# Attention in three score visits a pair, with one value product a pair from packed turned weights, and small operations joined

## The chip, the cores and the metric

One core of a Trainium2 chip runs the whole kernel. The time is what one execution takes on the device, in microseconds (us); the numbers below are medians of several executions, and one more execution was taken with the hardware profiler on. The core's engines work side by side and meet at semaphores: TensorE (PE) multiplies matrices into PSUM, eight banks of 128 x 512 float32; VectorE (DVE) and ScalarE (ACT) read PSUM and do elementwise work; GpSimd (POOL) fills and makes masks; SyncE's queue (SP) issues the large loads. Each engine works through its instructions in order.

## The reference

Two decoder layers on 512 tokens of width 1024, in float32. Layer 0 has an attention mixer with 16 heads of 64, layer 1 a gated short convolution; each is followed by a gated MLP of width 2816 with a causal width-3 convolution. Only the attention is touched:

```python
proj = rms_norm(h, norm_g) @ w_in          # q, k, v of 16 heads and 8 forget logits
q_fox = rms_norm(q[:, :H_FOX], fox_q_g)    # likewise k_fox, q_sb, k_sb: per head
# heads 0-7, forgetting attention
logits = q @ k.T * dh ** -0.5 + cum_f[q] - cum_f[k]
o = softmax(where(key_pos <= q_pos, logits, -inf)) @ v
# heads 8-15, stick-breaking attention
z = q @ k.T * dh ** -0.5
log_one_minus = where(key_pos < q_pos, log_sigmoid(-z), 0)
later = reverse_cumsum(log_one_minus) - log_one_minus
o = where(key_pos < q_pos, exp(log_sigmoid(z) + later), 0) @ v
h = h + concat(o_fox, o_sb) @ w_out
```

A block of 128 queries needs only the keys up to its own end: 128, 256, 384 and 512 of them.

## The kernel before

**Number form.** Products need more than one pass of the 32-bit matmul format, so each operand is split into a high and a low part (tiles `*_hi`, `*_lo`): ACT copies to the high part, DVE subtracts it. `mm3` (L246) issues high x high, low x high, high x low; `load` (L210) does the same for weights when they arrive. A value product takes the weights of the softmax in two parts against a `v` tile that holds high and low side by side in 128 columns (L482).

**Pairs and visits.** Heads go in pairs `p` = 0..7 (0 to 3 forgetting, "fox"; 4 to 7 stick-breaking), the two heads on 64 partitions each. `logits(p, b)` (L597) is one visit: the scores of query block `b` for both heads, one PSUM bank each of the four with tag "b", then the softmax, or two sigmoids and a reverse product scan, into tiles `w`. With 64 rows a matmul uses half of the array, and the two heads' matmuls run side by side. The smallest width is 256 columns. `turn(p, b, ws)` (L645) transposes the weights on PE in a bank of tag "c" (two banks) and splits them into `pt` tiles, which hold 256 queries for each of 4 key blocks, with the part after the diagonal filled with zeros by GpSimd (L653). `weigh(p, half)` (L666) multiplies 256 queries with `v` into a bank of tag "a" (two banks) and adds the two column halves for each head into `o`.

**Fillers.** `queries_keys(p)` (L520) and `values(g)` (L482) are generators that project queries, keys and values of later pairs, into banks of tag "a". After its two sums, `queries_keys` has a chain: squares summed on PE (`sums`, L533), turned (`turned_sums`, L545), inverse root on DVE (`rsqrt`, L318), spread and turned again (`rows`, L571). `output(g, done)` (L692), also with tag "a", is half of the output projection; `output_begin` (L718) starts the last half in banks of tag "b".

**Order of the work.** The order is written out in Python: `fill(us)` (L192) adds to a quota and draws that much planned PE time from the fillers, `spend` (L179) moves a planned clock, and `after(us, fn)` (L184) issues a step when that clock has gone on so far. `SUMS, FLAT, ROWS` (L45) are the delays of the chain above, `FILL1, FILL2, BEFORE` (L47) the quotas around a visit. The main loop (L839) issues for each g the scores of block g, `FILL1`, the product of a half that was turned an iteration before, the turn of block g - 1, and `FILL2`. The compiler may still exchange instructions of one engine where their operands are ready at other times.

Of the kernel before, what the change touches and what calls it, by code (L numbers as in the profile page):

```python
# [25 lines left out]
P = 128  # L26
# [18 lines left out]
SUMS, FLAT, ROWS = 3.0, 1.5, 5.0  # L45
NSUMS, NROWS, LATE = 4.0, 3.0, 7.0
FILL1, FILL2, BEFORE = 1.0, 2.6, 2.0  # L47
# [3 lines left out]
def trunk(  # L51
# [24 lines left out]
    blank = tiny.tile([P, P], BF16, tag="blank", name="blank", bufs=1)  # L76
# [3 lines left out]
    xin_scope = ExitStack()  # L80
    xin = xin_scope.enter_context(tc.tile_pool(name="xin", bufs=1))
# [177 lines left out]
    class Norm:  # L259
# [25 lines left out]
        def scale(self, sums):  # L285
            v = tiny.tile([P, NB], F32, tag="nv", name=f"nv_{self.name}")
# [31 lines left out]
    def rsqrt(dst, v, n, name):  # L318

        def t(tag, dt=F32):  # L320
            return tiny.tile([P, n], dt, tag=f"{tag}{n}", name=f"{tag}_{name}")
# [49 lines left out]
    for g, ps_ in enumerate(((1, 2), (3, 4), (5, 6), (7,))):  # L371
# [110 lines left out]
    def values(g):  # L482
# [3 lines left out]
        for b in range(NB):  # L486
            acc = bank("a")
# [19 lines left out]
    rx2 = const.tile([P, NB], F32, tag="rx2", name="rx2")  # L507

    def square_norm():
        dve.tensor_tensor(rx2, norm.col, norm.col, op=ALU.mult)  # L510
        dve.tensor_scalar(rx2, rx2, 1.0 / HD, None, op0=ALU.mult)
# [8 lines left out]
    def queries_keys(p):  # L520
# [3 lines left out]
        v = tiny.tile([P, NB, 2, 2], F32, tag="qv", name=f"qv{p}")  # L524
        r = tiny.tile([P, NB, 2, 2], F32, tag="qr", name=f"qr{p}")
# [7 lines left out]
        def sums():  # L533
# [7 lines left out]
            flat = work.tile([P, 2 * P], F32, tag="flat", name=f"flat{p}", bufs=1)  # L541
# [3 lines left out]
        def turned_sums(t, flat):  # L545
            for i in range(2):
                pe.transpose(t[:, (2 + i) * P:(3 + i) * P], flat[:, i * P:(i + 1) * P], ident)
            spend(0.25)
            dve.tensor_tensor(
                v, t[:, 2 * P:4 * P].rearrange("p (i b c) -> p b i c", i=2, b=NB)[:, :, :, 0:2],  # L550
                rx2[:, :, None, None].to_broadcast([P, NB, 2, 2]), op=ALU.mult,
            )
            scales()

        def scales():
            vf, rf = (t.rearrange("p b i h -> p (b i h)") for t in (v, r))
            dve.tensor_scalar(vf, vf, EPS, None, op0=ALU.add)
            rsqrt(rf, vf, 16, f"qk{p}")
            rf = r.rearrange("p b i h -> p b (i h)")
            dve.tensor_tensor(rf, rf, norm.col[:, :, None].to_broadcast([P, NB, 4]), op=ALU.mult)  # L560
            if not fox:
                s = q_scale[p] = aw.tile([P, 2, NB, 2], F32, tag="qscale", name=f"qscale{p}", bufs=3)
                dve.tensor_copy(s[:, 0], r[:, :, 1, :])
                dve.tensor_scalar(s[:, 1], r[:, :, 1, :], -1.0, None, op0=ALU.mult)
            wides = {}
            for i in kept:
                wides[i] = work.tile([P, S], F32, tag="u0", name=f"qwide{p}{i}").rearrange("p (b h d) -> p b h d", b=NB, h=2)
                dve.tensor_copy(wides[i], r[:, :, i, :][:, :, :, None].to_broadcast([P, NB, 2, HD]))
# [12 lines left out]
        for i in range(2):  # L581
            acc = bank("a")
# [14 lines left out]
    def logits(p, b):  # L597
# [5 lines left out]
        n = (b + 1) * P  # L603
        wide = max(n, 256)
        tok = slice(b * P, n)
        ss = [bank("b") for _ in range(2)]
        for step, (ql, kl) in enumerate(((q_hi, k_hi), (q_hi, k_lo), (q_lo, k_hi))):
            for e in range(2):
                rows = slice(e * HD, (e + 1) * HD)
                pe.matmul(ss[e][:, 0:wide], ql[rows, tok], kl[rows, 0:wide], start=step == 0, stop=not fox and step == 2)  # L610
        if fox:
            for e in range(2):
                rows = slice(e * HD, (e + 1) * HD)
                pe.matmul(ss[e][:, 0:wide], dl[rows, p, tok], dr[rows, 0:wide], start=False, stop=False)
            for e in range(2):
                pe.matmul(ss[e][:, tok], ident16, mask, start=False, stop=True)
        spend((4 if fox else 3) * wide * 0.00044 + (0.12 if fox else 0))
        ws = []
        for e in range(2):
            s = ss[e]  # L620
            w = aw.tile([P, S], F32, tag="w", name=f"w{p}{b}{e}", bufs=WB)
            ws.append(w)
            if fox:
                top = tiny.tile([P, 1], F32, tag="top", name=f"top{p}{b}{e}")
                dve.reduce_max(top, s[:, 0:n], axis=AX.X, negate=True)
                total = tiny.tile([P, 1], F32, tag="total", name=f"total{p}{b}{e}")
                act.activation(w[:, 0:n], s[:, 0:n], AF.Exp, bias=top, accum_out=total)
                inv = tiny.tile([P, 1], F32, tag="inv", name=f"inv{p}{b}{e}")
                dve.reciprocal(inv, total)
                dve.tensor_scalar(w[:, 0:n], w[:, 0:n], inv, None, op0=ALU.mult)  # L630
            else:
                scale = q_scale[p]
                rest = aw.tile([P, S], F32, tag="rest", name=f"rest{p}{b}{e}")
                act.activation(rest[:, 0:n], s[:, 0:n], AF.Sigmoid, scale=scale[:, 1, b, e:e + 1])
                act.activation(w[:, 0:n - 1], s[:, 0:n - 1], AF.Sigmoid, scale=scale[:, 0, b, e:e + 1])

                pool.memset(w[:, n - 1:n], 0.0)
                back = rest[:, 1:n][:, ::-1]
                dve.tensor_tensor_scan(back, back, begin[:, S - n + 1:S][:, ::-1], 0.0, op0=ALU.mult, op1=ALU.max)  # L639
                dve.tensor_tensor(w[:, 0:n - 1], w[:, 0:n - 1], rest[:, 1:n], op=ALU.mult)  # L640
        return ws
# [3 lines left out]
    def turn(p, b, ws):  # L645

        half, n = b // 2, (b + 1) * P
        if b % 2 == 0:
            pts[p, half] = []
            for e in range(2):  # L650
                both = [aw.tile([P, NB, 256], F32R, tag=f"pt{i}", name=f"pt{p}{half}{e}{i}", bufs=PT) for i in range(2)]
                for t in both:
                    pool.memset(f32(t[:, 2 * half + 1, 0:P]), 0.0)  # L653
                pts[p, half].append(both)
        at_ = slice((b % 2) * P, (b % 2 + 1) * P)
        for e in range(2):
            t = bank("c")
            for k in range(b + 1):
                pe.transpose(t[:, k * P:(k + 1) * P], ws[e][:, k * P:(k + 1) * P], ident)  # L659
            src = t[:, 0:n].rearrange("p (k q) -> p k q", q=P)  # L660
            hi, lo = pts[p, half][e]
            act.activation(hi[:, 0:b + 1, at_], src, AF.Copy)
            dve.tensor_tensor(lo[:, 0:b + 1, at_], src, f32(hi[:, 0:b + 1, at_]), op=ALU.subtract)
        spend(0.22 * (b + 1))

    def weigh(p, half):  # L666
# [4 lines left out]
        acc = bank("a")  # L671
        to = slice(half * 256, (half + 1) * 256)
        last = 2 * half + 1
        for e in range(2):
            hi, lo = pts[p, half][e]
            for k in range(last + 1):
                w = v[:, k, 2 * (p % 2) + e].rearrange("p i d -> p (i d)")
                pe.matmul(acc[:, e * 256:(e + 1) * 256], w, hi[:, k, :], start=k == 0, stop=False)
                pe.matmul(acc[:, e * 256:(e + 1) * 256], w, lo[:, k, :], start=False, stop=k == last)
        spend(0.44 * (last + 1))  # L680
        if p == 4 and half == 0:
            o_tiles[1] = mixed(1)
        o_hi, o_lo = o_tiles[p // 4]
        total = work.tile([P, S], F32, tag="y", name=f"o{p}{half}")[:, 0:256]
        for e in range(2):
            own, other = (slice(i * HD, (i + 1) * HD) for i in (e, 1 - e))
            cols = slice(e * 256, (e + 1) * 256)
            act.activation(total[own, :], acc[other, cols], AF.Copy)
            dve.tensor_tensor(total[own, :], acc[own, cols], total[own, :], op=ALU.add)  # L689
        split(o_hi[:, p % 4, to], o_lo[:, p % 4, to], total)  # L690
# [120 lines left out]
    after(NORM0, lambda: (norm.scale(sums0), square_norm()))  # L811
# [6 lines left out]
    aw = attn.enter_context(tc.tile_pool(name="aw", bufs=2))  # L818

# [5 lines left out]
    dr = ap_.tile([P, S], F32R, tag="dr", name="dr")  # L825
# [6 lines left out]
    for g, ps_ in enumerate(((1, 2), (3, 4), (5, 6), (7,))):  # L832
# [3 lines left out]
    blocks = [(p, b) for p in range(8) for b in range(NB)]  # L836
    waiting = {}
    fill(PRE)
    for g in range(len(blocks) + 2):  # L839
        if g < len(blocks):  # L840
            waiting[g] = logits(*blocks[g])
            fill(FILL1)
        if g == len(blocks):
            fillers.append(output_begin())
            fill(BEFORE)
        if g >= 2 and blocks[g - 2][1] % 2:
            p, b = blocks[g - 2]
            weigh(p, b // 2)
            if (p, b) == (3, 3):
                fillers.append(output(0, residual))  # L850
        if 1 <= g <= len(blocks):
# [161 lines left out]
```

## Time and profile before

| | us |
|---|---|
| median of 3 runs | 1221.25 (1220.8 to 1221.3) |
| profiled execution, its own time | 1220.77 |
| its span, first to last instruction | 1219.0 |
| PE busy in the span | 1204.0 |
| DVE, ACT, POOL busy | 762.8, 503.4, 26.6 |
| attention stage, roughly | 35 to 285 us of the span |

In the profile's rows, a line such as L610 is a line of the kernel; PE stands for matmuls and PEld for their weight loads. The end of a matmul is modelled, so the time of one is best read from the start of one to the start of the next. Tiles stand by name without their buffer numbers: psa, psb and psc are PSUM banks of the tags "a", "b" and "c".

### The profile page before, as it was taken

Reading aid. Unit: us, or ns where it says so; the run is one execution under the profiler, and the core shown is the slowest. Engines: PE = TensorE matmul, PEld = TensorE weight load, DVE = VectorE, ACT = ScalarE, POOL = GpSimd, SP = SyncE. Lnnn points to the kernel's source line nnn. Section 1 sums busy time; section 2 is a strip of 40 time slices with the busy share of each in tenths; the row PEclk is TensorE's granted clock in tenths of the full one; section 3 lists DMA queues with packets and bytes.
Section 4 is the critical chain, followed back from the end, with each engine's and each line's share of the span. In section 5 each row is a group of like instructions: output and inputs, shape, how many; then the busy total and the mean of one; then the engine's idle time right before and its main releaser. Section 6 shows DMA issues by size and latency. Waiting matters only on the chain.

```text
span 1219.0 us, 15006 instructions
## 1 busy us (share of the span) xinstructions
PE 1204.0 (99%) x5841; PEld 973.4 (80%) x5841; DVE 762.8 (63%) x1250; ACT 503.4 (41%) x787; POOL 26.6 (2%) x139
## 2 busy tenths in 40 slices
PE   8999999999999999999999999999999999999998
PEld 7887877778888888888888888888888888888886
DVE  5887888887867777663333555465776767672222
ACT  6556576655544443432222222233434344442120
POOL 4000000000000000000000000000000000000000
PEclk9999999999999999999999999999999999999999
DMA  7312121213233333323333333323233332322330
GB/s 196 88 36 70 36 69 36 70 62 96 87 102 89 97 93 94 96 81 93 94 95 104 89 102 87 104 87 104 87 93 98 89 102 87 103 87 88 121 102 35
DMA packets 182696, 108.14 MB, mean 89 GB/s; under 512 B 4732, under 2 KB 175020, under 8 KB 182624
## 3 DMA queue, kind: packets, MB, share of 16 engines
q1 hardware_dynamic: 182080, 106.94, 29.7%
q8 instruction: 46, 0.75, 0.3%
q0 software_dynamic: 384, 0.17, 0.1%
q14 instruction: 26, 0.21, 0.1%
q10 hardware_dynamic: 160, 0.07, 0.0%
HBM read 105.06 MB, written 2.10 MB: 88 GB/s over the span
## 4 chain that ended last, share of the span: by engine, by line
PE 91%; DVE 6%; ACT 2%; issue 1%; DMA 0%; SPq 0%; DVEq 0%; POOL 0%; ACTq 0%
PE psa L248 13%; PE psa L250 12%; PE psa L249 12%; PE psb L248 12%; PE psb L250 12%; PE psb L249 12%; PE psa L503 2%; PE psa L504 2%; PE psa L505 2%; PE psb L504 2%; PE psb L503 2%; PE psb L505 2%; DVE rest L639 1%; PE psc L659 1%; PE psb L610 1%
## 5 line engine op out<-in xcount | busy, mean ns | idle before, releaser
L227 ACT ACTIVATE whi<-raw 128x1024 fp32r<-128x1024 f32 (+3 forms) x199 | 208.9, 1050 | 362.7 <-PE psb L249 134.9
L228 DVE TENSOR_TENSOR wlo<-raw,whi 128x1024 fp32r<-128x1024 f32 (+3 forms) x199 | 240.4, 1209 | 160.2 <-ACT whi L227 159.1
L248 PE MATMUL psa<-hs_hi,whi 128*128 128x512 f32 x544 | 219.4, 403 | 2.5 <-DVE o L689 1.3
L250 PE MATMUL psa<-hs_hi,wlo 128*128 128x512 f32 x544 | 215.1, 395 | 0.2 <-DVE wlo L228 0.2
L249 PE MATMUL psa<-hs_lo,whi 128*128 128x512 f32 x544 | 214.6, 395 | 0.0
L248 PE MATMUL psb<-hs_hi,whi 128*128 128x512 f32 x480 | 189.9, 396 | 0.0
L250 PE MATMUL psb<-hs_hi,wlo 128*128 128x512 f32 x480 | 189.8, 395 | 0.0
L249 PE MATMUL psb<-hs_lo,whi 128*128 128x512 f32 x480 | 188.7, 393 | 0.0
L347 DVE SCALAR_TENSOR_TENSOR u<-y,taps,u 128x510 f32<-128x510 f32 (+1 forms) x176 | 131.1, 748 | 3.3 <-ACT u L344 0.4
L248 PEld LDWEIGHTS psa<-hs_hi,whi 128*128 128x128 f32 x544 | 102.3, 188 | 25.7 <-issue 2.3
L250 PEld LDWEIGHTS psa<-hs_hi,wlo 128*128 128x128 f32 x544 | 102.2, 188 | 25.0 <-DVE wlo L228 1.1
L249 PEld LDWEIGHTS psa<-hs_lo,whi 128*128 128x128 f32 x544 | 102.3, 188 | 22.2 <-DVE hs_lo L758 0.4
L249 PEld LDWEIGHTS psb<-hs_lo,whi 128*128 128x128 f32 x480 | 90.1, 188 | 21.4
L250 PEld LDWEIGHTS psb<-hs_hi,wlo 128*128 128x128 f32 x480 | 90.1, 188 | 21.4
L248 PEld LDWEIGHTS psb<-hs_hi,whi 128*128 128x128 f32 x480 | 90.3, 188 | 20.2
L885 DVE TENSOR_TENSOR y<-psb,nrow_n 128x512 f32<-128x512 f32 x44 | 30.4, 691 | 83.3 <-PE psb L250 83.3
L339 ACT ACTIVATE a<-u 128x512 fp32r<-128x512 f32 x44 | 27.9, 634 | 118.7 <-DVE u L890 118.7
L889 ACT ACTIVATE u<-u 128x512 f32<-128x512 f32 x44 | 27.9, 633 | 91.3 <-DVE u L347 91.3
L344 ACT ACTIVATE u<-y,taps 128x512 f32<-128x512 f32 x88 | 63.1, 719 | 1.2 <-DVE y L885 1.1
L340 DVE TENSOR_TENSOR a<-u,a 128x512 fp32r<-128x512 f32 x44 | 30.5, 692 | 29.4 <-ACT a L339 29.4
L503 PE MATMUL psa<-whi,hs_hi 128*128 128x256 f32 (+1 forms) x128 | 38.3, 299 | 0.8 <-ACT qk L593 0.7
L505 PE MATMUL psa<-whi,hs_lo 128*128 128x256 f32 (+1 forms) x128 | 36.3, 283 | 0.0
(251 smaller groups left out, 1818.3 us busy)
## 6 DMA issues: line engine op xcount, KB each, us to landing
raw<-in_ffn_w_up SPq DMA_DIRECT2D x88, 512.0 KB, 3.8
raw<-in_ffn_w_down SPq DMA_DIRECT2D x30, 512.0 KB, 3.7
raw<-in_attn_w_in SPq DMA_DIRECT2D x24, 512.0 KB, 4.0
raw<-in_conv_w_in SPq DMA_DIRECT2D x24, 512.0 KB, 3.8
raw<-in_ffn_w_down SPq DMA_DIRECT2D x16, 448.0 KB, 3.6
raw<-in_attn_w_out SPq DMA_DIRECT2D x8, 512.0 KB, 3.5
raw<-in_conv_w_out SPq DMA_DIRECT2D x8, 512.0 KB, 3.9
x_tok<-in_x SPq DMA_DIRECT2D x4, 512.0 KB, 6.5
```

The source lines that it names most:

```text
L227: return (act.activation(hi[:, at_], raw[:, at_], AF.Copy), dve.tensor_tensor(lo[:, at_], raw[:, at_], f32(hi[:, at_]), op=ALU.subtract))
L228: dve.tensor_tensor(lo[:, at_], raw[:, at_], f32(hi[:, at_]), op=ALU.subtract))
L248: made = [pe.matmul(acc, w[0], rhs[0], start=first, stop=False), pe.matmul(acc, w[0], rhs[1], start=False, stop=False), pe.matmul(acc, w[1 ...
L249: pe.matmul(acc, w[0], rhs[1], start=False, stop=False),
L250: pe.matmul(acc, w[1], rhs[0], start=False, stop=last)]
L340: dve.tensor_tensor(lo, src, f32(hi), op=ALU.subtract)
L344: act.activation(dst, src, AF.Copy, scale=tap(2))
L347: dve.scalar_tensor_tensor(dst[:, d:], src[:, 0:S - d], tap(j), dst[:, d:], op0=ALU.mult, op1=ALU.add)
L503: pe.matmul(acc, lhs[0], w[0], start=first, stop=False)
L504: pe.matmul(acc, lhs[0], w[1], start=False, stop=False)
L505: pe.matmul(acc, lhs[1], w[0], start=False, stop=last)
L885: dve.tensor_tensor(y, acc, norm.row, op=ALU.mult)
```

## The change

**Visits.** The query blocks of a pair come in three visits, `UNITS = (0, 1), (2,), (3,)`. The first has blocks 0 and 1 in one bank per head, in columns 0 to 255 and 256 to 511, each with matmuls of 256 columns as before. The tile `w` holds both heads. Where a visit has two blocks, reciprocals and multiplications are joined over the heads.

**Turned weights.** A pair has one tile of 20 blocks of 128 x 128 for the high parts and one for the low parts: the ten blocks on and under the diagonal for each of two heads, so that nothing is filled with zeros. For query blocks 0 and 1 both heads go through one bank and one copy.

**Value product.** `weigh(p)` runs once a pair. For key block k it takes the queries from block k on: 512, 384, 256 and 128 columns, from strided blocks. Each head has its own bank of tag "a".

**Small operations.** The normalization's factor drops out of the q and k scales, since they are normalized per head: in its place EPS is scaled by the mean square. Two operations in the chain become one.

**Order and places.** Queries, keys and values after the first go to banks of tag "b". `ROWS` is 8.0 in place of 5.0, `FILL1` 1.5 in place of 1.0, `FILL2` 3.3 in place of 2.6, per visit. The groups of fillers are (1, 2), (3, 4, 5), (6, 7), () in place of (1, 2), (3, 4), (5, 6), (7,). `dr` shares a tile with the stick-breaking `rest`, and `flat` with `nrow`.

```diff
-SUMS, FLAT, ROWS = 3.0, 1.5, 5.0
+SUMS, FLAT, ROWS = 3.0, 1.5, 8.0
-FILL1, FILL2, BEFORE = 1.0, 2.6, 2.0
+FILL1, FILL2, BEFORE = 1.5, 3.3, 2.0
+UNITS = (0, 1), (2,), (3,)
...
-            acc = bank("a")
+            acc = bank("b" if g >= 1 else "a")
...
-            acc = bank("a")
+            acc = bank("b" if p >= 1 else "a")
...
+        def scores(ql, kl, first, last):
+            for b, n, c, _ in parts:
+                wide = max(n, 256)
+                for e in range(2):
+                    rows = slice(e * HD, (e + 1) * HD)
+                    pe.matmul(ss[e][:, c:c + wide], ql[rows, b * P:n], kl[rows, 0:wide], start=first and b == bs[0], stop=last and b == bs[-1])
+
+        scores(q_hi, k_hi, True, False)
+        scores(q_hi, k_lo, False, False)
+        scores(q_lo, k_hi, False, not fox)
+        if fox:
+            scores(dl[:, p, :], dr, False, False)
+            for e in range(2):
+                for b, n, c, _ in parts:
+                    pe.matmul(ss[e][:, c + b * P:c + n], ident16, mask, start=False, stop=b == bs[-1])
...
+            for es in at_once(u):
+                dve.reciprocal(inv[:, :, es], total[:, :, es])
...
-                rest = aw.tile([P, S], F32, tag="rest", name=f"rest{p}{b}{e}")
+            rest = rests[0]
...
+                        act.activation(rest[:, e, keys], ss[e][:, c:c + n], AF.Sigmoid, scale=scale[:, 1, b, e:e + 1])
+                        act.activation(own[j][:, e, :], ss[e][:, c:c + n], AF.Sigmoid, scale=scale[:, 0, b, e:e + 1])
+                        back = rest[:, e, keys][:, ::-1]
+                        dve.tensor_tensor_scan(back, back, begin[:, S - n:S][:, ::-1], 0.0, op0=ALU.mult, op1=ALU.max)
...
-                for t in both:
-                    pool.memset(f32(t[:, 2 * half + 1, 0:P]), 0.0)
...
+        if b == 0:
+            pts[p] = [aw.tile([P, 20, P], F32R, tag=f"pt{i}", name=f"pt{p}{i}", bufs=1) for i in range(2)]
...
-        for e in range(2):
-            hi, lo = pts[p, half][e]
-            for k in range(last + 1):
-                w = v[:, k, 2 * (p % 2) + e].rearrange("p i d -> p (i d)")
-                pe.matmul(acc[:, e * 256:(e + 1) * 256], w, hi[:, k, :], start=k == 0, stop=False)
-                pe.matmul(acc[:, e * 256:(e + 1) * 256], w, lo[:, k, :], start=False, stop=k == last)
...
         for e in range(2):
+            acc = bank("a")
+            for k in range(NB):
+                w = v[:, k, 2 * (p % 2) + e].rearrange("p i d -> p (i d)")
+                first, step = ((6 * k, 5), (1 + k, 6))[e]
+                out_ = acc[:, k * P:] if e == 0 else acc[:, 0:(NB - k) * P]
+                for i, t in enumerate(pts[p]):
+                    pe.matmul(out_, w, t[:, first:first + step * (NB - k - 1) + 1:step, :], start=k == 0 and i == 0, stop=k == NB - 1 and i == 1)
...
+            act.activation(to, src[other], AF.Copy)
+            dve.tensor_tensor(to, src[own], to, op=ALU.add)
+            spend(1.2)
+        split(o_hi[:, p % 4, :], o_lo[:, p % 4, :], total)
```

More of the change, by code (lines that the diff above doesn't have):

```diff
@@ L370, in trunk @@
     want_qk(0)
-    for g, ps_ in enumerate(((1, 2), (3, 4), (5, 6), (7,))):
+    for g, ps_ in enumerate(((1, 2), (3, 4, 5), (6, 7), ())):
         if g == 0:
@@ L505, in mm3_rhs, with least_square @@
         pe.matmul(acc, lhs[1], w[0], start=False, stop=last)
[L507 to L511, printed above, removed]
+    least = const.tile([P, 2 * NB], F32, tag="least", name="least")
+    def least_square():
+        for i in range(2):
+            dve.tensor_scalar(least[:, i * NB:(i + 1) * NB], norm.mean, EPS, None, op0=ALU.mult)
     halves, q_scale, done = {}, {}, set()
@@ L540, in sums @@
             spend(0.6)
-            flat = work.tile([P, 2 * P], F32, tag="flat", name=f"flat{p}", bufs=1)
+            flat = work.tile([P, S], F32, tag="nrow", name=f"flat{p}", bufs=1)[:, 0:2 * P]
             act.activation(flat, t[:, 0:2 * P], AF.Copy)
@@ L603, in logits, with turn @@
+        return [(b, x) for (b, n, c, a), x in zip(parts, own)]
+    pts = {}
+    def turn(p, b, w):
         n = (b + 1) * P
[L604 to L607, printed above, removed]
+        if b == 0:
+            pts[p] = [aw.tile([P, 20, P], F32R, tag=f"pt{i}", name=f"pt{p}{i}", bufs=1) for i in range(2)]
+        if b < 2:
+            t = bank("c")
             for e in range(2):
-                rows = slice(e * HD, (e + 1) * HD)
-                pe.matmul(ss[e][:, 0:wide], ql[rows, tok], kl[rows, 0:wide], start=step == 0, stop=not fox and step == 2)
@@ L611, in logits @@
-        if fox:
-            for e in range(2):
-                rows = slice(e * HD, (e + 1) * HD)
-                pe.matmul(ss[e][:, 0:wide], dl[rows, p, tok], dr[rows, 0:wide], start=False, stop=False)
-            for e in range(2):
[L616 to L632, printed above, removed]
-                rest = aw.tile([P, S], F32, tag="rest", name=f"rest{p}{b}{e}")
[L634 to L640, printed above, removed]
@@ L641, in logits @@
-        return ws
-    pts = {}
[L645 to L651, printed above, removed]
-                for t in both:
-                    pool.memset(f32(t[:, 2 * half + 1, 0:P]), 0.0)
[L654 to L660, printed above, removed]
-            hi, lo = pts[p, half][e]
-            act.activation(hi[:, 0:b + 1, at_], src, AF.Copy)
-            dve.tensor_tensor(lo[:, 0:b + 1, at_], src, f32(hi[:, 0:b + 1, at_]), op=ALU.subtract)
+                for k in range(b + 1):
+                    c = (e * (b + 1) + k) * P
+                    pe.transpose(t[:, c:c + P], w[:, e, k * P:(k + 1) * P], ident)
@@ new lines, in turn @@
+            src = t[:, 0:2 * n].rearrange("p (e n) -> p e n", e=2)
+            if b:
+                hi, lo = (t_[:, 4:20, :].rearrange("p (e k) q -> p e (k q)", e=2)[:, :, P:3 * P] for t_ in pts[p])
+            else:
+                hi, lo = (t_[:, 0:20:19, :] for t_ in pts[p])
+            act.activation(hi, src, AF.Copy)
+            dve.tensor_tensor(lo, src, f32(hi), op=ALU.subtract)
+        else:
+            for e in range(2):
+                t = bank("c")
+                for k in range(b + 1):
+                    pe.transpose(t[:, k * P:(k + 1) * P], w[:, e, k * P:(k + 1) * P], ident)
+                to = (5 * b, 19 - 6 * b)[e]
+                hi, lo = (t_[:, to:to + b + 1, :].rearrange("p k q -> p (k q)") for t_ in pts[p])
+                act.activation(hi, t[:, 0:n], AF.Copy)
+                dve.tensor_tensor(lo, t[:, 0:n], f32(hi), op=ALU.subtract)
@@ L664, in turn, with weigh @@
         spend(0.22 * (b + 1))
-    def weigh(p, half):
+    def weigh(p):
         need(("v", p // 2))
         v = v_tiles[p // 2]
[L671 to L675, printed above, removed]
-            for k in range(last + 1):
-                w = v[:, k, 2 * (p % 2) + e].rearrange("p i d -> p (i d)")
[L678 to L681, printed above, removed]
+        if p == 4:
@@ L682, in weigh @@
             o_tiles[1] = mixed(1)
         o_hi, o_lo = o_tiles[p // 4]
-        total = work.tile([P, S], F32, tag="y", name=f"o{p}{half}")[:, 0:256]
+        total = work.tile([P, S], F32, tag="y", name=f"o{p}")
         for e in range(2):
-            own, other = (slice(i * HD, (i + 1) * HD) for i in (e, 1 - e))
-            cols = slice(e * 256, (e + 1) * 256)
-            act.activation(total[own, :], acc[other, cols], AF.Copy)
-            dve.tensor_tensor(total[own, :], acc[own, cols], total[own, :], op=ALU.add)
@@ L835, in trunk @@
             fillers.append(values(g + 1))
-    blocks = [(p, b) for p in range(8) for b in range(NB)]
+    units = [(p, u) for p in range(8) for u in range(len(UNITS))]
     waiting = {}
     fill(PRE)
-    for g in range(len(blocks) + 2):
-        if g < len(blocks):
-            waiting[g] = logits(*blocks[g])
+    for g in range(len(units) + 2):
+        if g < len(units):
+            waiting[g] = logits(*units[g])
             fill(FILL1)
-        if g == len(blocks):
+        if g == len(units):
             fillers.append(output_begin())
             fill(BEFORE)
[L846 to L849, printed above, removed]
+        if g >= 2 and units[g - 2][1] == len(UNITS) - 1:
+            p = units[g - 2][0]
+            weigh(p)
+            if p == 3:
                 fillers.append(output(0, residual))
-        if 1 <= g <= len(blocks):
-            turn(*blocks[g - 1], waiting.pop(g - 1))
-            fill(FILL2)
+        if 1 <= g <= len(units):
+            for b, w in waiting.pop(g - 1):
+                turn(units[g - 1][0], b, w)
+                fill(FILL2 / len(UNITS[units[g - 1][1]]))
     fill(1e9)
```

80 lines of the change are left out of this document (59 added, 21 removed).

## The prediction, made blind

> **What bounds the kernel now.** The page of the profile was read first: the span, the busy shares and the chain that ended last.
>
> ```profile
> span 1219.0 us, 15006 instructions
> ...
> PE 1204.0 (99%) x5841; PEld 973.4 (80%) x5841; DVE 762.8 (63%) x1250; ACT 503.4 (41%) x787; POOL 26.6 (2%) x139
> ...
> PE 91%; DVE 6%; ACT 2%; issue 1%; DMA 0%; SPq 0%; DVEq 0%; POOL 0%; ACTq 0%
> ```
>
> TensorE (PE) is the bound, so what counts is the time that its stream takes. Matmul ends are modelled, so a busy share of 99% does not say that each matmul runs at its best rate; for that I read start to start in the timeline. The second view is the table of stretches: the attention stage, and for comparison a stretch of the first MLP.
>
> ```profile
> core 0: us, PE busy (x) PEld busy (x) DVE busy (x) ACT busy (x) POOL busy (x), PEclk, DMA share, GB/s
> 50.00:275.00 225.00, 217.10 (x1460) 173.64 (x1459) 184.80 (x462) 139.99 (x318) 13.81 (x92) 1.00 0.19 55
> ...
> 300.00:400.00 100.00, 100.00 (x439) 81.17 (x438) 73.25 (x104) 43.15 (x56) 0.00 (x0) 1.00 0.33 96
> ```
>
> The MLP has no PE gap, and nothing of it is edited. The attention stage has 225 - 217.1 = 7.9 us of PE gaps, VectorE (DVE) busy 82% of it, ScalarE (ACT) 62%. The third view says who PE waited for from 35 to 275 us (time in all, times, longest):
>
> ```profile
> PE psc L659 <- DVE pt L663: 1.7, 2, 1.4
> PE psa L248 <- DVE o L689: 1.6, 2, 1.3
> PE psc L575 <- DVE pt L663: 1.4, 2, 0.9
> PE psa L248 <- DVE h L727: 1.3, 1, 1.3
> ...
> PE psc L575 <- DVE qwide L568: 0.5, 1, 0.5
> ...
> PE psa L503 <- ACT qk L593: 0.3, 1, 0.3
> ```
>
> So three things can move the end: PE work, PE's changes between tile shapes, and these 7.9 us. All other engines matter only through the third.
>
> **Term 1, one score visit fewer per pair.** The scores use half the array's rows (64 of 128), two heads side by side. This is what one visit costs between full matmuls (start, busy, what):
>
> ```profile
> 219.03 0.40 PE L250 MATMUL psa<-hs_hi,wlo 128*128 128x512 f32 x1
> 219.35 0.39 PE L610 MATMUL psb<-qk_hi,qk_hi 64*128 64x256 f32 x2
> 219.58 0.28 PE L610 MATMUL psb<-qk_lo,qk_hi 64*128 64x256 f32 x2
> 219.69 0.28 PE L610 MATMUL psb<-qk_hi,qk_lo 64*128 64x256 f32 x2
> 219.91 0.50 PE L248 MATMUL psa<-hs_hi,whi 128*128 128x512 f32 x1
> 220.24 0.39 PE L249 MATMUL psa<-hs_lo,whi 128*128 128x512 f32 x1
> ```
>
> From 219.03 to 220.24 stand 1.21 us. In them are two full matmuls of 512 columns, 0.23 us each start to start (222.53 to 222.76 below), and three pairs of 256 columns, 0.11 us each (219.58 to 219.69): 0.79 us of work. The other 0.42 us are lost at the two changes of shape, about 0.1 us at each of the four affected starts. The count of visits follows from the groups by shape, two heads to a visit:
>
> ```profile
> L610 PE MATMUL psb<-qk_hi,qk_hi 64*128 64x256 f32 x32 | 6.4, 376 | 0.0
> ...
> L610 PE MATMUL psb<-qk_hi,qk_hi 64*128 64x512 f32 x16 | 4.0, 496 | 0.0
> ...
> L610 PE MATMUL psb<-qk_hi,qk_hi 64*128 64x384 f32 x16 | 3.5, 439 | 0.0
> ```
>
> (32 + 16 + 16)/2 = 32 visits. The change makes it 24. The joined visit issues the same matmuls of the same widths (two blocks of 256 columns each, four starts a step in place of two), the decay and mask matmuls too, so nothing but the change of shape goes: 8 x 0.42 = 3.4 us. Bounds: 0, if filler matmuls are put between the halves of a joined visit, which then changes shape as often as two visits do, and 3.4 us. I take 3.4, since the halves' operands are ready together.
>
> **Term 2, the value product.** Now a pair issues 8 + 16 = 24 matmuls of 256 columns, zero blocks included. Sixteen of them:
>
> ```profile
> 222.53 0.39 PE L249 MATMUL psa<-hs_lo,whi 128*128 128x512 f32 x1
> 222.76 0.37 PE L678 MATMUL psa<-pt,v 128*128 128x256 f32 x1
> ...
> 224.64 0.28 PE L679 MATMUL psa<-pt,v 128*128 128x256 f32 x1
> 224.76 0.39 PE L250 MATMUL psa<-hs_hi,wlo 128*128 128x512 f32 x1
> ```
>
> The last takes 0.12 us, 24 of them 2.88 us. After, each of two heads has high and low products of 512, 384, 256 and 128 columns. 512 costs 0.23, 256 0.12, 384 lies between (0.175). The narrowest is not in the trace as such a product; the nearest rows are the transposes, 128 columns with a weight load each:
>
> ```profile
> 215.60 1.04 PE L659 MATMUL psc<-ident,w 128*128 128x128 f32 x8
> 216.39 0.48 PE L248 MATMUL psa<-hs_hi,whi 128*128 128x512 f32 x1
> 216.71 0.39 PE L249 MATMUL psa<-hs_lo,whi 128*128 128x512 f32 x1
> ```
>
> Eight transposes and one full matmul from 215.60 to 216.71: 1.11 - 0.23 = 0.88, 0.11 us each. Bounds for a narrow product: 0.06 (half of a 256-column one) and 0.12 (no cheaper than it). I take 0.11. A pair then costs 4 x (0.23 + 0.175 + 0.12 + 0.11) = 2.54 us, 0.34 less, in 8 pairs 2.7 us (with the bounds 2.4 to 4.3). Skipped blocks of an access pattern in the moving operand are not in these rows; runs stay 128 elements long, so I price them at nothing.
>
> The Trainium skill, page "TensorE: Matmul & The Clock Gate", section "Back-to-back issue gap", gives some 81 ns a matmul for 128 columns in a stream of loads and matmuls, where the transposes here take 110. By the page the 32 narrow products would save 0.9 us more and the forecast would be 1211.5; the sum goes by the transposes.
>
> **Term 3, the waits.** Four edits bear on the 7.9 us. (a) Query, key and value sums after the first move from the two psa banks to the four psb banks, so they no longer wait for the product's evacuation: the 1.6 us of psa behind L689 and 0.3 us behind L593 go. (b) ROWS 5 to 8 puts the row turns (L575) 3 us of planned work later; their waits were 0.9 us at most, so 1.4 + 0.5 go. (c) The planned filler work between a visit's scores and its turn rises from 1.0 + 2.6 + 1.0 = 4.6 us to 1.5 + 3.3 + 1.5 = 6.3 us, and a pair takes 6 psc banks for turns in place of 8: of the 1.7 us of L659 I take half, 0.9. That is 4.7 us. (d) Against it: the product now asks for two psa banks, one per head, and while the first half of the output projection (L727's psa) is suspended with a bank half summed, the second head waits until ACT and DVE have emptied the first one's. Their durations are bounded by 512-column rows:
>
> ```profile
> L663 DVE TENSOR_TENSOR pt<-psc,pt 128x512 fp32r<-128x512 f32 x16 | 10.6, 686 | 1.4 <-ACT pt L662 1.3
> ...
> L593 ACT ACTIVATE qk<-psa,head_gains 128x512 f32<-128x512 f32 x12 | 8.3, 689 | 0.0
> ```
>
> 0.69 + 0.69 = 1.4 us; by the filler quota two products fall into that time, less what is hidden: 1.7 us back. Net 3.0. Bounds: 7.9 us gained (no gap left), 5 us lost (the product's 1.4 us at three or four of the pairs, gaps as before).
>
> **At nothing:** the joined small operations. Per pair some ten DVE instructions go (two subtractions of turned weights, two head additions, a split, two small scaling operations, three reciprocals or two multiplications):
>
> ```profile
> L629 DVE RECIPROCAL inv<-total 128x1 f32<-128x1 f32 x32 | 4.9, 159 | 2.4 <-ACT w L627 2.4
> ```
>
> At 0.16 us for one with hardly an element, 80 of them are 13 us of DVE's 184.8, which lie beside PE's work and are worth only what term 3 already has. The zero fills on GpSimd go likewise. **The end of the stage** costs a little: one product of 2.5 us for the whole pair stands at the end where 1.9 us stood, its copies are twice as wide, and the last slack was
>
> ```profile
> 278.76 0.42 DVE L340 TENSOR_TENSOR o_lo<-o,o_hi 128x256 fp32r<-128x256 f32 x1 [0.49 <-ACT o_hi L339]
> ...
> 279.86 0.39 PE L248 MATMUL psb<-o_hi,whi 128*128 128x512 f32 x1
> ```
>
> 0.7 us. Two wider copies and two wider splits take about 0.3 us each longer, but the first head's run beside the second's matmuls: 0.3 us lost. If that cover goes, 1.
>
> **Sum.** 3.4 + 2.7 + 3.0 - 0.3 = 8.8 us off the profiled execution's 1220.77 (its span is 1219.0): 1212.0. The runs' median is 1221.25, 0.5 above that execution: forecast 1212.4.
>
> **Rivals.** First, the joined visit is late, and PE waits at its turn. Rows of a stick-breaking visit:
>
> ```profile
> L639 DVE TENSOR_TENSOR_SCAN rest<-rest,begin 128x255 f32<-128x255 f32 x8 | 5.3, 678 | 2.2 <-ACT rest L634 2.2
> ...
> L634 ACT ACTIVATE rest<-psb,qscale 128x256 f32<-128x256 f32 x8 | 3.9, 486 | 3.2 <-PE psb L610 2.7 <-DVE w L640 0.5
> ...
> L634 ACT ACTIVATE rest<-psb,qscale 128x128 f32<-128x128 f32 x8 | 2.9, 368 | 2.0 <-PE psb L610 2.0
> ```
>
> ACT has four sigmoids at each width, 4 x (0.49 + 0.37) = 3.4 us, then one scan of 0.68 and the joined multiplications, some 1.1 (estimated from 0.69 for 512 elements): 5.2 us, and with one weight split on each of ACT and DVE ahead of it 7.5:
>
> ```profile
> L227 ACT ACTIVATE whi<-raw 128x1024 fp32r<-128x1024 f32 (+3 forms) x199 | 208.9, 1050 | 362.7 <-PE psb L249 134.9
> L228 DVE TENSOR_TENSOR wlo<-raw,whi 128x1024 fp32r<-128x1024 f32 (+3 forms) x199 | 240.4, 1209 | 160.2 <-ACT whi L227 159.1
> ```
>
> The cover is 6.3 us and the scores and turns between, some 1.3. It is even, so it can fail: late by 1.1 us at each of 8 pairs, it eats the 8.8 us: 1221. Against it: under the shorter cover of now no wait of PE in the table above is for scores turned to weights too late (its L659 waits are for the bank that L663 empties).
>
> Engines do take turns at a bank here. In the copies after the product, where both heads share one, the waits have
>
> ```profile
> ACT o L688 <- DVE o L689: 6.1, 7, 1.8
> ```
>
> The Trainium skill, page "PSUM — Partial Sum Buffer", section "Terms", has it as a rule that no two engines may be on one bank at once. By it a joined forgetting visit, with DVE's maximum of one block and ACT's exponential of the other in one bank, would also run late, and the time would be this rival's 1221. The row agrees with the rule, but no time of PE hangs on it, so the chance stays as it is.
>
> Second, slower: the psb banks. Scores, and now 14 query and key sums and 12 value sums, share four. If a filler's first matmul finds none free until ACT has squared and copied the sum before (0.60 and 0.69 us), PE waits 1.3 us at 14 sums, 18 us: 1212.4 + 18 = 1230. It decides from a mean wait of 8.8/26 = 0.34 us a sum. For it: such waits exist today on psa. Against: waits behind L593 are 0.3 us in all, with only two banks.
>
> Third, a larger gain: all 7.9 us of gaps go and narrow products take 0.06: 1220.8 - 3.4 - 4.3 - 7.9 + 0.5 = about 1206.
>
> **Chances.** Forecast (1208 to 1217) 0.67; larger gain 0.09; late joined visit, within some 3 us of the time before, 0.12; the banks 0.12. A measurement here can tell about 0.2%, 2.4 us, from no change. Faster: 0.67 + 0.09 and a sixth of the late case, 0.78; same 0.10; slower 0.12. Range: from a little below the larger gain, 1205, to the late visit's better half, 1220; outside lie the banks, and half of the late case.
>
> **What would show it.** Right: 24 visits of scores with about 0.4 us lost at each; 128 products of values, 128-column ones 0.11 us apart; PE gaps of about 5 us in the attention stage, none at L575's successor behind DVE; no psb sum waiting for ACT. Wrong: PE waiting for turned weights after joined visits, gaps ahead of psb sums, narrow products as long as wide ones, or a gap where the last quarter of the output projection starts.

## The result

| | median, us | runs | profiled execution, us (span) |
|---|---|---|---|
| before | 1221.28 | 4 | 1220.77 (1219.0) |
| changed | 1206.22 (1206.01 to 1206.50) | 4 | 1206.01 (1204.2) |

The ratio is 0.9877, with a 95% interval of 0.9863 to 0.9892: 15.1 us faster, where 8.8 were forecast. The time is inside the stated range, 1.2 us from its end, but outside the forecast's own band of 1208 to 1217, and within 0.3 us of the rival of a larger gain. In this section and the next, "the changed kernel" is 1206.2.

The page of the changed kernel: the span, the busy shares and the chain.

```profile
span 1204.2 us, 14562 instructions
...
PE 1194.2 (99%) x5777; PEld 969.8 (81%) x5777; DVE 751.3 (62%) x1174; ACT 496.1 (41%) x747; POOL 12.7 (1%) x48
...
PE 93%; DVE 5%; ACT 1%; DMA 0%; issue 0%; DVEq 0%; SPq 0%; ACTq 0%
```

PE is still the bound and has 64 matmuls fewer: 8 a pair, the value product. The table of stretches for the same 50 to 275 us and for the MLP:

```profile
50.00:275.00 225.00, 221.68 (x1464) 181.74 (x1463) 185.14 (x402) 140.74 (x290) 0.44 (x5) 1.00 0.20 59
...
300.00:400.00 100.00, 100.00 (x432) 80.89 (x431) 73.25 (x93) 42.22 (x56) 0.00 (x0) 1.00 0.33 96
```

PE's gaps there are 225 - 221.7 = 3.3 us, before 7.9. DVE has 402 instructions in place of 462, but the same busy time, since the stretch now holds more of the kernel. GpSimd is nearly empty (0.44 us). What PE still waits for (35 to 275 us: time, times, longest):

```profile
PE psc L574 <- DVE pt L698: 1.4, 1, 1.4
PE psc L541 <- DVE pt L698: 1.1, 2, 0.7
PE psa L718 <- DVE o L725: 0.5, 1, 0.5
PE psa L718 <- DVE h L764: 0.2, 1, 0.2
```

(L574 turns the scale rows, L541 sums squares, L694 and L682 turn weights, L698 subtracts turned weights, L718 is the value product, L622 the scores.) Three waits, 2.5 us in all, are for a psc bank that DVE has yet to empty. The product's waits for a psa bank are there, as step (d) had them, at under half its price. None is for a psb bank and none for weights of a joined visit.

One joined visit and one product in the timeline:

```profile
223.12 0.39 PE L251 MATMUL psa<-o_hi,wlo 128*128 128x512 f32 x1
223.44 0.51 PE L622 MATMUL psb<-qk_hi,qk_hi 64*128 64x256 f32 x4
223.78 0.40 PE L622 MATMUL psb<-qk_lo,qk_hi 64*128 64x256 f32 x4
224.01 0.40 PE L622 MATMUL psb<-qk_hi,qk_lo 64*128 64x256 f32 x4
224.34 0.50 PE L249 MATMUL psa<-o_hi,whi 128*128 128x512 f32 x1
224.68 0.40 PE L250 MATMUL psa<-o_lo,whi 128*128 128x512 f32 x1
...
158.31 2.66 PE L718 MATMUL psa<-pt,v 128*128 128x512 f32 x16
160.80 0.62 PE L574 MATMUL psc<-ident,qwide 128*128 128x128 f32 x4
```

The visit takes 1.56 us from 223.12 to 224.68; the work in it is 2 x 0.23 + 6 x 0.115 = 1.15 us, so 0.41 us is lost, as much as at a visit of one block. The product of a pair takes 160.80 - 158.31 = 2.49 us, where 24 matmuls of 0.12 came to 2.88.

**The account by the trace.** Counted in the timeline of the attention stage, runs of half-array matmuls begin 27 times in place of 38: eight visits less, and three fewer visits split by fillers: 11 x 0.41 = 4.5 us. The products: 8 x 0.39 = 3.1 us. PE's gaps: 7.9 - 3.3 = 4.6 us. A gap is shown about 0.16 us too short, because the modelled end of a 512-column matmul stands 0.39 us after its start, and the next may start after 0.23; starts that come over 0.15 us late behind a shown gap went from 16 to 8, which adds 1.3 us. (Taken from the starts alone, these waits were 10.7 us and are 4.6, so 6.1 less.) Together 13.5 of the spans' 14.8 us; 1.3 us are in no term.

### The profile page after: what moved, and what is told of

Its sections match the earlier page's. It is cut to its first block, busy times and chain, and to the rows that moved or that the text cites. A ratio compares the mean times of both kernels' runs of the same rounds, so it can differ in the third digit from the quotient of the medians.

```text
span 1204.2 us, 14562 instructions
## 1 busy us (share of the span) xinstructions
PE 1194.2 (99%) x5777; PEld 969.8 (81%) x5777; DVE 751.3 (62%) x1174; ACT 496.1 (41%) x747; POOL 12.7 (1%) x48
## 4 chain that ended last, share of the span: by engine, by line
PE 93%; DVE 5%; ACT 1%; DMA 0%; issue 0%; DVEq 0%; SPq 0%; ACTq 0%
PE psb L249 14%; PE psb L251 14%; PE psb L250 14%; PE psa L249 11%; PE psa L251 11%; PE psa L250 11%; PE psb L504 2%; PE psb L505 2%; PE psb L506 2%; PE psa L504 2%; PE psa L505 2%; PE psa L506 2%; PE psb L622 1%; PE psa L718 1%; DVE rest L663 1%; DVE wlo L229 1%
## 5 line engine op out<-in xcount | busy, mean ns | idle before, releaser
L249 PE MATMUL psb<-hs_hi,whi 128*128 128x512 f32 x592 | 237.4, 401 | 0.0
L251 PE MATMUL psb<-hs_hi,wlo 128*128 128x512 f32 x592 | 234.0, 395 | 0.0
L250 PE MATMUL psb<-hs_lo,whi 128*128 128x512 f32 x592 | 232.8, 393 | 0.0
L249 PE MATMUL psa<-hs_hi,whi 128*128 128x512 f32 x432 | 171.5, 397 | 0.9 <-ACT whi L228 0.9
L251 PE MATMUL psa<-hs_hi,wlo 128*128 128x512 f32 x432 | 170.8, 395 | 0.3 <-DVE wlo L229 0.2
L250 PE MATMUL psa<-hs_lo,whi 128*128 128x512 f32 x432 | 170.4, 394 | 0.0
L250 PEld LDWEIGHTS psb<-hs_lo,whi 128*128 128x128 f32 x592 | 111.3, 188 | 24.6
L250 PEld LDWEIGHTS psa<-hs_lo,whi 128*128 128x128 f32 x432 | 81.1, 188 | 19.3 <-DVE hs_lo L795 0.4
L504 PE MATMUL psa<-whi,a 128*128 128x512 f32 x88 | 35.5, 403 | 0.0
L504 PE MATMUL psb<-whi,a 128*128 128x512 f32 x88 | 34.9, 396 | 0.0
```

Source lines behind the costliest of these rows:

```text
L249: made = [pe.matmul(acc, w[0], rhs[0], start=first, stop=False), pe.matmul(acc, w[0], rhs[1], start=False, stop=False), pe.matmul(acc, w[1 ...
L250: pe.matmul(acc, w[0], rhs[1], start=False, stop=False),
L251: pe.matmul(acc, w[1], rhs[0], start=False, stop=last)]
L504: pe.matmul(acc, lhs[0], w[0], start=first, stop=False)
```

## The experiments

All were timed beside the kernel before (1221.1 to 1221.2 in their series); ratios are to it. Their 95% intervals are about 1.7 us either way, so a difference of under some 2 us between two series is a hint, which the traces can support, and no more. Theory: visits, product and waits add up, as the prediction had them, with sizes to be found. Rivals: the longer cover alone; the banks alone; DVE's shorter chains.

**Four visits again.**

```diff
-UNITS = (0, 1), (2,), (3,)
+UNITS = (0,), (1,), (2,), (3,)
-FILL1, FILL2, BEFORE = 1.5, 3.3, 2.0
+FILL1, FILL2, BEFORE = 1.0, 2.6, 2.0
```

> The changed kernel (1206.2 us), but with four visits a pair again, one block each, and the filler quotas per visit of before (1.0 and 2.6), so that the planned filler work in all is the same; packed turned weights, the narrow products and the banks stay as changed. If the visits are worth what the changes of array shape cost (0.42 us lost at each of 8 visits), this run is 3.4 us slower than the changed kernel, 1209.6, and if visits are also split by fillers as before, up to 1210.5. The rival says that the gain beyond the forecast comes from the longer cover between a visit's scores and its turn: then this run gives back 6 us or more, over 1212, and the added time stands in PE gaps, not at changes of shape. If filler order alone decides, it stays within 1 us of 1206.2.

Measured 1209.37, ratio 0.9904 (0.9891 to 0.9918): 3.2 us slower than the changed kernel, as the changes of shape had it. The table of stretches agrees (50 to 260 us, PE busy second):

```profile
50.00:260.00 210.00, 207.72 (x1384) 167.34 (x1383) 175.67 (x399) 132.51 (x278) 0.44 (x5) 1.00 0.20 56
```

The gaps are 2.3 us, fewer than the changed kernel's 3.3 in the same stretch, with half-array runs beginning 36 times: nine more starts of 0.41 us are 3.7 us, less 1.0 us of gaps. The rival had 6 us or more, all in gaps, and falls. The cover was not changed without the visits, so its own worth stays unmeasured.

**Key, query and value sums back in psa.**

```diff
-            acc = bank("b" if g >= 1 else "a")
+            acc = bank("a")
...
-            acc = bank("b" if p >= 1 else "a")
+            acc = bank("a")
```

> The changed kernel, but query, key and value sums go to the two banks of tag a again, which the product now asks for twice a pair. By the prediction's step (a) the waits of 1.6 us behind the head additions and of 0.3 us behind the query copies come back: 1.9 us, 1208.1. A larger share of the unforeseen gain lies here if the run is above 1210, since the product with two banks a pair then blocks every filler. If the banks did not matter, 1206.2.

Measured 1217.13 (1214.27 to 1218.54), ratio 0.9964 (0.9952 to 0.9977): 10.9 us lost, nearly six times the price of step (a). Not all of that is waiting: the five runs go from 1214.27 at a granted clock of 1.000 to 1218.54 at 0.996, so the loss is 8.1 us where the clock held. PE's waits and the stretch in the profiled execution (1218.54), which has 8.4 us of gaps and a granted clock of 0.98:

```profile
PE psa L718 <- DVE o L725: 2.9, 2, 2.4
PE psa L718 <- DVE v L498: 2.1, 2, 1.9
PE psc L574 <- DVE pt L698: 1.3, 1, 1.3
PE psa L718 <- ACT qk L592: 1.3, 1, 1.3
...
```

```profile
50.00:260.00 210.00, 201.65 (x1337) 163.57 (x1336) 167.70 (x379) 129.69 (x274) 0.44 (x5) 0.98 0.18 54
```

The product stands at the end of every wait for psa. For 2.9 us it waits for the first head's bank, which is the mechanism of step (d); for 3.4 us it waits for a bank in which a filler's finished sum (L498, L592) has yet to be copied out. Half-array runs begin 32 times in place of 27, another 2.1 us. Without the bank move the rest of the change gains 4.1 us in place of 15.1.

**The bank move alone, in the kernel before** (the same two lines there).

> The kernel before with one edit alone: query, key and value sums after the first go to the four banks of tag b. The changed kernel lost 10.9 us when this edit was undone. If the edit is worth its own waits (1.6 us behind the head additions, 0.3 us behind the query copies), the run is 1.9 us faster than before, 1219.3; if it is what makes the gain in general, it is some 8 us faster, 1213; and if the four banks then block the scores, it is slower than 1222. The first is my theory: the 10.9 us come only with the product that holds both a banks.

Measured 1216.57, ratio 0.9962 (0.9949 to 0.9976): 4.7 us faster than before, between the first two expectations, so the theory's 1.9 us was too small. The banks alone are under a third of the change. The stretch from 50 to 260 us, first of the kernel before, then of this run:

```profile
50.00:260.00 210.00, 202.10 (x1381) 161.48 (x1380) 173.15 (x444) 131.91 (x304) 13.05 (x88) 1.00 0.19 54
```

```profile
50.00:260.00 210.00, 204.29 (x1401) 164.34 (x1401) 175.97 (x449) 132.89 (x307) 13.36 (x88) 1.00 0.19 56
```

The gaps are 5.7 us after 7.9, and half-array runs begin 35 times in place of 38, 1.2 us. So the edit pays twice: in the wait, and in order, since fewer visits are split. That a filler's late bank is what splits them is inferred from the two coming together.

**ROWS back to 5.**

```diff
-SUMS, FLAT, ROWS = 3.0, 1.5, 8.0
+SUMS, FLAT, ROWS = 3.0, 1.5, 5.0
```

> The changed kernel with ROWS at 5.0 as before. By step (b) the turns of the scale rows come 3 us of planned work too early again and wait for DVE: 1.9 us, 1208.1. The rival says that other edits (fewer DVE instructions, fewer banks of tag c) had already taken these waits away: 1206.2 within 0.5.

Measured 1208.05, ratio 0.9893 (0.9880 to 0.9907): 1.8 us lost, where step (b) has 1.9. Its longest waits:

```profile
PE psc L694 <- DVE qn L576: 2.2, 2, 1.7
PE psc L574 <- DVE qwide L567: 1.4, 3, 1.0
...
```

The row turn waits for the chain on DVE (L567), and turned weights for its bank. That is not quite step (b): of its 1.9 us, 1.4 were a wait for a bank that turned weights held, and 0.5 for the chain.

**ROWS 8 alone, in the kernel before** (the same line).

> The kernel before with ROWS at 8.0 alone. By step (b) the row turns' 1.9 us of waits go: 1219.3. The rival: in the kernel before the waits there were for the turned weights of the visits (DVE's L663), not for the rows themselves, so a later turn only moves them: 1221.2 within 1.

Measured 1221.5, ratio 1.0003 (0.9994 to 1.0011): no change, so the rival holds here. The waits at row turns are down to 0.3 us, and others are longer:

```profile
PE psc L659 <- DVE pt L663: 2.2, 1, 2.2
PE psc L539 <- DVE pt L663: 1.8, 2, 1.3
PE psa L248 <- DVE o L689: 1.3, 2, 0.9
PE psa L503 <- DVE o L689: 0.9, 1, 0.9
PE psc L539 <- ACT sq L585: 0.5, 1, 0.5
PE psc L659 <- DVE qv L549: 0.4, 1, 0.4
PE psc L575 <- DVE pt L663: 0.3, 1, 0.3
...
```

The same edit is worth 1.8 us in one kernel and nothing in the other, where the wait moved. Part of that is the clock: the two of eleven runs with a granted clock of 1.000 took 1220.0 and 1220.5, the four at 0.996 or 0.997 took 1222.5 to 1222.9.

**Wide products.**

```diff
-            for k in range(NB):
...
-                for i, t in enumerate(pts[p]):
-                    pe.matmul(out_, w, t[:, first:first + step * (NB - k - 1) + 1:step, :], start=k == 0 and i == 0, stop=k == NB - 1 and i == 1)
+            for half in range(2):
+                for k in range(2 * half + 2):
...
+                    for i, t in enumerate(pts[p]):
+                        pe.matmul(acc[:, half * 256:(half + 1) * 256], w, t[:, first:first + 6:5, :], start=k == 0 and i == 0, stop=k == 2 * half + 1 and i == 1)
```

> The changed kernel with 24 value matmuls of 256 columns a pair in place of 16 of 512 to 128, still one bank a head; they read other blocks of the packed tiles, so this run's values after the attention are not the reference's. By term 2 of the prediction the product is 2.7 us dearer (2.4 by the starts in the changed kernel's trace): 1208.6 to 1208.9. If the product's length is hidden by something else, 1206.2; if the narrow products also gave a gain in waits, over 1210.

Measured 1208.52, ratio 0.9898 (0.9883 to 0.9913): 2.3 us, term 2 within 0.4.

**The joined operations apart.** Once all of them, then each half.

```diff
-        return (slice(0, 2),) if u == 0 else (slice(0, 1), slice(1, 2))
+        return (slice(0, 1), slice(1, 2))
...
-        if b < 2:
+        if b < 0:
             t = bank("c")
```

> The changed kernel with the joined operations of the first visit taken apart again: reciprocals and multiplications per head, turned weights of blocks 0 and 1 copied and subtracted per head out of one bank each. The packed tiles, visits and products stay. The prediction priced the joining at nothing, since it lies beside PE's work: 1206.2 to 1206.7. The rival says that the shorter DVE and ACT chains are what took the waits from 10 to 4 us: then this run is 3 us or more slower, above 1209, with PE waiting for DVE's subtractions of turned weights.

Measured 1209.81, ratio 0.9907 (0.9893 to 0.9920): 3.6 us lost. "At nothing" was wrong, and the rival's time, above 1209, came. The first line alone (weights apart), and the second alone (turns apart):

> The changed kernel with the reciprocals and multiplications of the first visit per head again, 2 more DVE instructions a pair at most; the turned weights stay joined. Taking both joinings apart cost 3.6 us. If DVE's time is what counts, this half carries a part in proportion to its DVE time, under 1 us: 1206.5 to 1207.2. If the cost lies in the psc banks that the turns take, this run is 1206.2 within 0.5.

> The changed kernel with blocks 0 and 1 turned per head again: 8 psc banks a pair in place of 6, and two more copies and subtractions. If the psc banks are what counts, most of the 3.6 us is here: 1209 to 1210. If the instructions alone count, it is about half: 1208.

Weights apart: 1206.55, ratio 0.9878 (0.9864 to 0.9893), 0.3 us, not told from none. Turns apart: 1210.14, ratio 0.9909 (0.9892 to 0.9925), 3.9 us: all of it. Its waits:

```profile
PE psc L541 <- DVE pt L698: 1.5, 2, 1.0
PE psc L694 <- DVE pt L698: 1.4, 2, 0.7
PE psc L694 <- DVE qn L576: 0.6, 1, 0.6
PE psa L718 <- DVE o L725: 0.5, 1, 0.5
PE psc L574 <- DVE pt L698: 0.4, 1, 0.4
...
```

Those for psc come to 3.9 us, after the changed kernel's 2.5. By the starts in the trace, counted as above, there are 13 waits of 6.9 us in place of 8 of 4.6. Eight banks a pair are asked for, six with the joining. Two more copies and subtractions a pair come with it, so the run does not part the bank from the instructions that empty it. With the weights apart, up to two more DVE instructions a pair elsewhere cost nothing that can be told from none.

**First half of the output projection in psb.**

```diff
                 w = weights()
-            acc = bank("a")
+            acc = bank("b")
```

> The changed kernel with the first half of the output projection in banks of tag b too, so that the product alone has the two a banks. Step (d) says that the product waits for a half summed bank of the projection; in the changed kernel's trace such waits are 0.9 us. If they go, 1205.3; if the scores of the last pairs then find no bank of tag b, 1206.2 or more.

Measured 1205.62, ratio 0.9872 (0.9859 to 0.9886). The product's waits (0.7 us in the changed kernel's table, not the 0.9 of the expectation) are gone from the trace, one of 0.7 us has come at a psb bank; 0.6 us better than the changed kernel, less than two series can tell apart.

**The chain's banks in psa,** on top of that edit: row turns alone, then row turns and sums of squares.

```diff
             for i in kept:
-                t = bank("c")
+                t = bank("a" if p >= 1 else "c")
...
-            t = bank("c")
+            t = bank("a" if p >= 1 else "c")
             for i in range(2):
                 for b in range(NB):
                     pe.matmul(t[32 * b:32 * (b + 1), i * P:(i + 1) * P], head_ones, sqs[i][:, b * P:(b + 1) * P], start=True, stop=True)
```

> The changed kernel with the first half of the output projection in banks of tag b and the turns of the scale rows (after the first pair) in the two a banks, which the product then leaves idle most of the time. The changed kernel's longest PE wait, 1.4 us, is that turn waiting for a psc bank that DVE empties. If the two psc banks are the cause, the wait goes and the time is 1204 to 1204.5; if DVE itself is late, the wait moves to another bank: 1205.6, as with the projection alone.

> As the run before it, and the sums of squares also go to the a banks, so that turned weights have the two psc banks alone. PE's waits for those banks (1.4 and 1.1 us) should both go: 1203 to 1203.5. Against it: a sum holds its bank for the planned time to its turn, and a product that comes between finds one a bank only; then it is above 1206.

Row turns alone: 1206.35, ratio 0.9877 (0.9862 to 0.9892), 0.7 us over the run it builds on: the long wait, 1.4 us, has moved to a psa bank that the product's copies empty. The second expectation had such a move, though by a late DVE and with a time of 1205.6. Both: 1204.16 (1203.83 to 1204.69), ratio 0.9860 (0.9845 to 0.9875), the fastest of all, 2.1 us under the changed kernel, though the two intervals overlap, and 0.7 over what was expected. Its waits:

```profile
PE psa L574 <- DVE o L725: 1.6, 2, 1.4
PE psb L249 <- DVE v L498: 0.7, 1, 0.7
PE psb L622 <- ACT qk_hi L340: 0.2, 1, 0.2
```

No wait for psc is left; the row turns now wait for the product's banks, so only one of the two waits that should go went. These edits change banks and leave DVE's work as it was: what they gain speaks for the psc banks as the cause of the 3.9 us above, without proving it.

## Why the prediction was right in its way and too small

- **Term 1, visits.** Right: 0.42 us a visit forecast, 0.41 in the trace, 3.4 us forecast, 3.2 by undoing it (nine starts more and 1.0 us of gaps less). The joined visits stayed whole. Three visits fewer were split, which the term left out.
- **Term 2, product.** Right: 2.7 us forecast; 2.3 by the wide products, 3.1 by the trace. The narrow products run in twos with one weight tile: in the trace the second starts 0.06 us after the first, and the next product 0.11 after that, 0.085 on average for which I took 0.11. The strided blocks, priced at nothing, cost nothing that shows: 512, 384 and 256 columns take 0.23, 0.175 and 0.12 us start to start. The figure of the Trainium skill ("TensorE: Matmul & The Clock Gate", "Back-to-back issue gap", some 81 ns at 128 columns) was the nearer one.
- **Term 3, waits.** This is the step that failed, in size: net 3.0 us forecast, about 6 in the trace (4.6 of shown gaps and 1.3 under modelled ends). (a) The bank move was priced at the waits that named it, 1.9 us; alone it gave 4.7, of which 1.2 by fewer split visits, and with the new product it carries 10.9 (8.1 where the clock held). (b) ROWS at 1.9 us was right in number in the changed kernel (1.8), in part by luck, since the waits that came back are others, and would have been wrong alone (0). (c) Turned weights in six psc banks a pair were given 0.9 us; taking the joining apart cost 3.9. The cover, to which (c) gave part of that, shows no gain: four visits under the shorter cover have fewer gaps. (d) The product waiting for the projection's bank came true, at 0.7 us of shown waits where 1.7 were set down, and with the edit of psb 0.6 us went.
- **At nothing.** Right for reciprocals and multiplications (0.3 us). Wrong for the joined turns, which stood in (c) as banks and here as DVE time: they spare psc banks, which PE waits for most (2.5 of 3.2 us of its shown waits). The sum counted the waits that the table names and forgot that each is shown short and that one wait sets the place of the next.
- **End of the stage.** 0.3 us forecast. The last o_lo ends at 260.26 and PE has no gap there: nothing was lost.

```profile
259.57 0.69 DVE L341 TENSOR_TENSOR o_lo<-o,o_hi 128x512 fp32r<-128x512 f32 x1 [0.70 <-ACT o_hi L340]
```

- **Rivals.** No PE wait for joined weights: the late visit did not come. No psb wait: the slower case did not come, although a psb wait of 0.7 us appears as soon as the projection joins that tag. The larger gain is where the time fell, with less from gaps (6 us for 7.9) and from the product (3.1 for 4.3) and more from visits (4.5 for 3.4) than that rival had; that its sum lies so close is luck.

The parts do not add up: undone one by one they cost 3.2 + 10.9 + 1.8 + 2.3 + 3.6 = 21.8 us for a change worth 15.1, since the same wait is removed only if two edits are both there. What the 1.3 us outside the terms are stays open.

## What to carry to other kernels

Where the matrix engine is the bound and its gaps are few, price a change first by the engine's own work and its changes of array shape: these two terms came out within about 0.5 us when undone. Waits for PSUM banks are not priced by the row that names them: give a generator that can be suspended half summed a tag of its own, count the banks that each chain holds, and look first for joinings that also free a bank: here the one that did was worth 3.9 us, the one that only spared DVE's time nothing that could be told. Try an edit on order both alone and with its companions, for it can be worth nothing in one and some 2 us in the other.

## What the runs showed of the hardware

**A wait of 2.2 us was followed by a lower clock, which cost over half as much again.** In the run with ROWS 8 alone, PE stood still before the turn at 213.20:

```profile
213.20 1.58 PE L659 MATMUL psc<-ident,w 128*128 128x128 f32 x8 [2.23 <-DVE pt L663]
...
215.01 0.63 PE L249 MATMUL psa<-hs_lo,whi 128*128 128x512 f32 x1
215.43 0.63 PE L250 MATMUL psa<-hs_hi,wlo 128*128 128x512 f32 x1
215.86 0.63 PE L248 MATMUL psa<-hs_hi,whi 128*128 128x512 f32 x1
```

```profile
214.50:217.50 3.00, 3.00 (x10) 2.39 (x9) 3.00 (x8) 1.77 (x6) 0.10 (x1) 0.57 0.12 25
217.50:220.00 2.50, 2.50 (x13) 2.02 (x12) 2.50 (x6) 1.04 (x3) 0.00 (x0) 1.00 0.51 180
```

The matmuls after it start 0.43 us apart in place of 0.23, the granted clock is 0.57 from 214.5 to 217.5 (the column behind POOL) and 1.00 after. Over 3 us that is 1.3 us lost on top of the wait. The same is seen where the banks were put back, after a wait of 1.9 us that ended at 164.88 and one of 2.4 us that ended at 221.31:

```profile
160.00:180.00 20.00, 18.13 (x97) 14.62 (x95) 15.99 (x29) 12.30 (x22) 0.10 (x1) 0.91 0.19 53
...
220.00:225.00 5.00, 3.69 (x14) 3.50 (x15) 2.26 (x8) 1.21 (x3) 0.00 (x0) 0.58 0.00 0
225.00:230.00 5.00, 5.00 (x32) 4.47 (x31) 2.74 (x5) 1.47 (x3) 0.00 (x0) 0.73 0.00 0
```

The longest wait with ROWS back to 5, 1.7 us, and the changed kernel's, 1.4 us, left the clock at 1.00. The Trainium skill, page "TensorE: Matmul & The Clock Gate", section "Why this matters for your kernels", warns of idle gaps over some 3 us between bursts; here 1.9 us were enough once, and 2.2 and 2.4 once each.

**The change of array shape** costs about 0.1 us at each of the four starts it touches, whether a visit has three pairs of matmuls or six. The Trainium skill, page "TensorEngine Tiling (Array Packing)", section "Key Properties", says that a change of tiling mode drains the engine, without a figure; this is one.
